# A hybrid decoder layer: where one scan block's outputs stand, and how the last two row tiles are normalised and stored

## The chip, the cores and the metric

The kernel runs on one core of one Trainium2 chip. The core has a matrix engine (TensorE, PE in the profile, with PEld for its weight loads), a vector engine (VectorE, DVE), a scalar engine (ScalarE, ACT), GpSimd (POOL) and SyncE (SP), which issues most transfers. Each engine works through its own instructions in their order; semaphores make one wait for another. The metric is the device time of one execution in microseconds, the median of several runs.

## The reference

One layer over 1024 positions of width 1024, then a final norm, all in float32:

```python
xn = rmsnorm(h, norm_gain)
proj = xn @ w_in                              # 1024 x 3072
u_ssm, z_ssm, h_conv, b_conv, c_conv, z_conv = columns of proj, 512 each
y_ssm = s5_mixer(u_ssm, ...) * silu(z_ssm)    # 32 groups x 64 complex states, scan over positions,
                                              # Re(C s) + D u, gelu, then y * sigmoid(y @ w_glu + b_glu)
y_conv = b_conv * causal_conv3(c_conv * h_conv) * silu(z_conv)
h = h + concat(y_ssm, y_conv) @ w_out
return rmsnorm(h, final_norm_gain)            # h * rsqrt(mean(h*h) + eps) * gain, row by row
```

## The kernel before

Products run as three matmul passes over a high and a low part of each operand (`h`, `x`, `l` in `project`). The first stage loads and normalises x and projects the scan's input. Its order is a table written by hand (`START`) and isn't touched.

The second stage has 16 convolution units and four scan blocks of 8 groups. Its order is the table `ORDER` (L36). A number n is a unit: `conv_hc` or `conv_bz` of channel block n // 4 and half n % 2; units 4 and 5 are `conv_hc` of block 1, unit 6 is `conv_bz`. Of scan block b, `p` prepares coefficients on DVE (`ssm_prep`), `m` and `q` build matrices (`ssm_inject`, `ssm_lags`, tiles `ps_w` and `ps_k`), `i` scans (`ssm_in`, tile `ps_s`; run at high priority, so its work moves ahead in every engine's row), and `o` makes the outputs (`ssm_out`). `ssm_out` has, for each of two halves of the groups, 8 small products into a PSUM tile `ps_y` (L593, L594), then GELU steps on ACT and DVE (L598 to L602), and at its end a store to a scratch tensor in DRAM (L603). A scheduler gives each engine its row of instructions from this order, with the dependencies; the PE row follows it closely, and work of DVE and ACT is interleaved. `ps_w`, `ps_k`, `ps_s` and `ps_y` share the four banks of the PSUM pool `psm` in turn; the results of `project` have four banks of their own (`pmm`). Blocks with an even number keep their scratch (`u2`, `xa`, `xb`, `w1`) in parts of `ysb`, the odd ones in a pool, so block 2 reuses block 0's.

The third stage gates the scan's outputs (`glu`, `gate_z`) and prepares parts of `w_out`. The last stage multiplies by `w_out` with a seven-product scheme over pairs of row tiles (128 rows each) and halves of the columns: T1 to T4 and S1 to S4 are its sums and differences. It loops over four pairs j. A pair's two tiles are `xa` and `xb`, loaded with x as the residual; each product lands in PSUM, `add` (L823, DVE) adds it to a half of a tile (`lo_` and `hi_`, 512 columns), and `final_square` (L826, ACT) sums the squares of a finished half. `rsqrt_steps` (L92 to L98) makes the row factor r from these sums in nine small DVE steps, and `finish` (L842, L843) multiplies a tile by r and the gain `g2b` in one DVE instruction and stores it from SP. The second tile of the last pair goes another way: its final product is computed in two quarters of 256 columns, POOL multiplies each piece by the gain as it comes (`xg`, L879 and L886), and r is applied in halves, one on ACT (L890) and one on DVE (L891), each with a store of its own, from SP (L892) and from ACT's queue (L893).

Of the kernel before, what the change touches and what calls it, by code (L numbers as in the profile page):

```python
# [13 lines left out]
AF = mybir.ActivationFunctionType  # L14
ALU = mybir.AluOpType
MUL, ADD, SUB = ALU.mult, ALU.add, ALU.subtract
# [16 lines left out]
START = ("s0 w0 n0 c s1 W0 n1 W1 w1 t0 L0 g0 L1 U010hl x0 u010x. W2 s2 s3 W3 L2 n23 u20hx u30hx t1 L3 g1 u230l. s4 x1 s5 n45 "  # L33
         "U01231h u01lx. k00 p0 u11lx. k10 t2 u21lx. k20 u31lx. k30 d12 g2 s6 x2 s7 C n67 d12 U01232h u01232l t3 g3 d8 x3 u01232x. "
         "U01233h u03l p1 p2 u03x. k01 u13lx. k11 d u23lx. k21 u33lx. k31")
ORDER = "p0 0 1 2 m0 q0 i0 3 p1 4 o0 5 6 m1 q1 i1 7 p2 8 o1 9 m2 q2 i2 10 p3 11 o2 m3 q3 i3 12 13 o3 14 15"  # L36
MAGIC = 12582912.0
LOG2E = 1.4426950408889634

# [18 lines left out]
def hybrid_kernel(ctx: ExitStack, tc, x, norm_gain, w_in, a_re, a_im, log_dt, b_re, b_im,  # L58
                  c_re, c_im, d_skip, w_glu, b_glu, conv_w, w_out, final_gain, out):
    nc = tc.nc  # L60
    V, A, Q, PE = nc.vector, nc.scalar, nc.gpsimd, nc.tensor
# [10 lines left out]
    out_ci = out[0].rearrange("(c i) d -> c i d", i=T)  # L72
# [11 lines left out]
    ysb = big.tile([P, NB, L], F32, tag="ys", name="ysb")  # L84
# [3 lines left out]
    def rsqrt_steps(parts):  # L88

        vh, y, t = (const.tile([P, 1], F32, tag=f"rs_{q}", name=f"{q}_{rsqrt_steps.n}", bufs=4) for q in ("vh", "y", "t"))  # L90
        rsqrt_steps.n += 1
        ops = [lambda: V.tensor_scalar(vh, parts[0], 0.5 / D, 0.5 * EPS, MUL, ADD)]  # L92
        for part in parts[1:]:
            ops.append(lambda part=part: V.scalar_tensor_tensor(vh, part, 0.5 / D, vh, MUL, ADD))
        ops.append(lambda: V.tensor_scalar(y.bitcast(I32), vh.bitcast(I32), -0.5, 1593268703.0, MUL, ADD))
        for _ in range(3):
            ops.append(lambda: V.scalar_tensor_tensor(t, y, vh, y, MUL, MUL))
            ops.append(lambda: V.scalar_tensor_tensor(y, t, 1.5, y, SUB, MUL, reverse0=True))  # L98
        return ops, y
# [544 lines left out]
    prep, inj, lags, st = {}, {}, {}, {}  # L644
    for what in ORDER.split():
        n = int(what.lstrip("pmiqoz"))
# [42 lines left out]
    g2b = ph3.tile([P, D], F32, name="g2b", bufs=1)  # L689
# [34 lines left out]
    def rows(op, j, home):  # L724

        a, b = (slice(j * 256 + m * P, j * 256 + m * P + P) for m in range(2))
        view = {"A11": cy[:, :, a], "A21": cy[:, :, b], "A12": ysb[:, :, a], "A22": ysb[:, :, b]}
        home = home.rearrange("p m (k c) -> p m k c", k=NB)
        aq[op, j] = home
        if op[0] == "A":  # L730
            t = view[op]
        else:
            t = temp(f"{op}{j}").rearrange("p (k c) -> p k c", k=NB)
            one, two = {"S1": ("A21", "A22"), "S2": ("S1", "A11"), "S3": ("A11", "A21"), "S4": ("A12", "S2")}[op]
            one, two = (view[m] if m in view else aq["raw", m, j] for m in (one, two))
            V.tensor_tensor(t, one, two, ADD if op == "S1" else SUB)
            aq["raw", op, j] = t
        split(home[:, 0], home[:, 1], t)
# [69 lines left out]
    def load_res(j):  # L808
        for m in range(2):
            xr[j, m] = (ph3, wst)[m].tile([P, D], F32, tag="wr", name=f"xr{j}{m}", bufs=2)  # L810
            nc.sync.dma_start(xr[j, m], x_ci[:, 2 * j + m, :])

    lo_, hi_ = slice(0, 512), slice(512, D)

    def mult(ps, op_a, op_b, j, first, cols=slice(0, 512)):
        out_ = ps[:, 0:cols.stop - cols.start]
        for m, (p, q) in enumerate(((0, 0), (0, 1), (1, 0))):
            for k in range(NB):
                PE.matmul(out_, aq[op_a, j][:, p, k], bq[op_b, k][:, q, cols], start=first and m + k == 0,  # L819
                          stop=m == 2 and k == NB - 1, skip_group_check=True)  # L820

    def add(x, ps):
        V.tensor_tensor(x, x, ps, ADD)  # L823

    def final_square(x, acc):
        A.activation(temp(f"sq{final_square.n}")[:, 0:x.shape[-1]], x, AF.Square, accum_out=acc)  # L826
        final_square.n += 1
# [4 lines left out]
    def first_product(j):  # L832
        pw[j] = pmm.tile([P, 512], F32, tag="mm", name=f"ow{j}")
        mult(pw[j], "A11", "B11", j, True)
        add(xr[j, 0][:, lo_], pw[j])

    def finish(j, m, parts):
        x = xr[j, m]
        ops, r = rsqrt_steps(parts)
        for op in ops:  # L840
            op()
        V.scalar_tensor_tensor(x, x, r, g2b, MUL, MUL)  # L842
        nc.sync.dma_start(out_ci[:, 2 * j + m, :], x)  # L843
# [3 lines left out]
    for j in pairs:  # L847
        last = j == pairs[-1]
        xa, xb = xr[j, 0], xr[j, 1]
        part = ph3.tile([P, 5], F32, tag="ss2", name=f"ssp{j}")  # L850
        pz, px = (psm.tile([P, 512], F32, tag="sm", name=f"o{m}{j}") for m in "zx")
        if not last:
            load_res(j + 1)
        mult(pz, "S1", "T1", j, True)
        add(xb[:, hi_], pz)
        mult(pw[j], "S2", "T2", j, False)
        add(xa[:, hi_], pw[j])
        if not last:
            for op in ("A11", "S1", "S2", "S4", "S3", "A12", "A22"):
                rows(op, j + 1, next(homes_a))  # L860
        mult(pz, "S4", "B22", j, False)
        add(xa[:, hi_], pz)
        final_square(xa[:, hi_], part[:, 0:1])
        mult(pw[j], "S3", "T3", j, False)
        add(xb[:, hi_], pw[j])
        final_square(xb[:, hi_], part[:, 2:3])
        mult(px, "A12", "B21", j, True)
        add(xa[:, lo_], px)
        final_square(xa[:, lo_], part[:, 1:2])
        finish(j, 0, [part[:, 0:1], part[:, 1:2]])  # L870
        if not last:
            first_product(j + 1)
            mult(pw[j], "A22", "T4", j, False)
            add(xb[:, lo_], pw[j])
            final_square(xb[:, lo_], part[:, 3:4])
            finish(j, 1, [part[:, 2:3], part[:, 3:4]])
            continue
        xg = ysb[:, 0]
        Q.tensor_tensor(xg[:, hi_], xb[:, hi_], g2b[:, hi_], MUL)  # L879
        steps, r = rsqrt_steps([part[:, 2:3], part[:, 3:4], part[:, 4:5]])  # L880
        for q in range(2):
            c = slice(q * 256, q * 256 + 256)
            mult(pw[j][:, c], "A22", "T4", j, False, c)
            add(xb[:, c], pw[j][:, c])
            final_square(xb[:, c], part[:, 3 + q:4 + q])
            Q.tensor_tensor(xg[:, c], xb[:, c], g2b[:, c], MUL)  # L886
            steps.pop(0)()
        for step_ in steps:
            step_()
        A.activation(xb[:, hi_], xg[:, hi_], AF.Copy, scale=r)  # L890
        V.tensor_scalar_mul(xb[:, lo_], xg[:, lo_], r)  # L891
        nc.sync.dma_start(out_ci[:, 2 * j + 1, lo_], xb[:, lo_])  # L892
        nc.scalar.dma_start(out_ci[:, 2 * j + 1, hi_], xb[:, hi_])  # L893
    ph3.release()
    ph2.release()

# [28 lines left out]
```

## Time and profile before

| what | value |
|---|---|
| median of three runs (lowest, highest) | 437.37 us (437.13, 706.63) |
| the profiled execution | 435.54 us |
| its span, first to last instruction | 433.7 us |
| granted TensorE clock in it | 0.993 |
| PE, DVE, ACT, POOL busy | 96%, 76%, 42%, 7% |
| DMA, mean over the span | 113 GB/s |

The span is what the trace covers; the rest of an execution's time lies around it. Times in the rows count from the span's start. A row of the timeline has start, duration, engine, line, operation, output <- inputs, shape and count, and in brackets how long the engine had been idle before it and who ended that. "SPq" and "ACTq" are the parts of SP and ACT that issue transfers and wait on semaphores. The highest of the three runs stands far above the other two and plays no part in the median.

### The profile page before, as it was taken

What the parts mean: (1) busy time and instruction counts of PE and PEld (TensorE: products, weight loads), DVE (VectorE), ACT (ScalarE), POOL (GpSimd) and SP (SyncE); (2) the same over time, 40 slices, a digit from 0 to 9 for tenths busy, and PEclk for the clock granted to TensorE, in tenths of its full rate; (3) what the DMA queues carried; (4) which work ended last, traced back from release to release, by engine and by line L of the source; (5) the groups of instructions that cost most, each with busy time, mean ns of one, the idle gap of its engine ahead of it and who ended that gap; (6) DMA issues with size and microseconds to landing.
All of it is one profiled execution on the core that took longest, in us unless ns stands there. A gap on an engine that the chain in (4) does not pass through costs nothing. (4 is left out here: it accounts for less than half of the span.)

```text
span 433.7 us, 6302 instructions
## 1 busy us (share of the span) xinstructions
PE 418.2 (96%) x2226; PEld 358.1 (83%) x2226; DVE 331.2 (76%) x821; ACT 181.6 (42%) x322; POOL 32.0 (7%) x39
## 2 busy tenths in 40 slices
PE   8998999999997999999999999999999999999991
PEld 8898999888887888888888888888888888888881
DVE  4973888969989979986996928746456799977734
ACT  4754933074213245135324414647434654333121
POOL 0000003001020020100021000211202100000011
PEclk9999999999999999999999999999999999999997
DMA  7983005433260641254025422577534540333212
GB/s 240 251 256 80 19 2 158 134 91 105 54 166 3 175 116 47 77 147 146 6 47 147 117 81 75 180 200 237 122 109 74 143 123 2 117 125 103 92 48 99
DMA packets 49472, 48.97 MB, mean 113 GB/s; under 512 B 6696, under 2 KB 39488, under 8 KB 49440
## 3 DMA queue, kind: packets, MB, share of 16 engines
q1 hardware_dynamic: 47568, 45.16, 35.5%
q0 software_dynamic: 1728, 3.15, 4.2%
q8 instruction: 17, 0.28, 0.3%
q10 hardware_dynamic: 144, 0.26, 0.2%
q14 instruction: 15, 0.12, 0.1%
HBM read 31.65 MB, written 8.39 MB: 92 GB/s over the span
## 5 line engine op out<-in xcount | busy, mean ns | idle before, releaser
L826 ACT ACTIVATE sq<-xr 128x512 f32<-128x512 f32 (+1 forms) x17 | 10.3, 606 | 41.8 <-DVE xr L823 30.1
L641 POOL TENSOR_TENSOR cy<-cy,sg 128x512 f32<-128x512 f32 x8 | 13.8, 1725 | 187.8 <-DVE sg L640 154.9
L747 PE MATMUL glu<-shl,wg 128*128 128x512 f32 x96 | 21.9, 389 | 0.0
L747 PEld LDWEIGHTS glu<-shl,wg 128*128 128x128 f32 x96 | 18.0, 188 | 3.7
L224 DVE SCALAR_TENSOR_TENSOR xl<-ps_x,g,xh 128x256 fp32r<-128x256 f32 x32 | 12.9, 474 | 8.6 <-ACT xh L218 8.6
L230 PE MATMUL mm_u<-xh,whu 128*128 128x256 f32 x128 | 17.5, 288 | 1.7 <-ACT xh L218 1.7
L230 PEld LDWEIGHTS mm_u<-xh,whu 128*128 128x128 f32 x128 | 16.2, 191 | 2.4 <-ACT xh L218 2.1
L230 PE MATMUL mm_u<-xh,wlu 128*128 128x256 f32 x128 | 17.9, 285 | 0.0
L230 PE MATMUL mm_u<-xl,whu 128*128 128x256 f32 x128 | 17.5, 284 | 0.0
L819 PE MATMUL ow<-bs,ax 128*128 128x512 f32 (+1 forms) x54 | 16.9, 367 | 0.5 <-DVE xr L823 0.5
L230 PE MATMUL mm_h<-xh,wlh 128*128 128x512 f32 x64 | 16.5, 394 | 0.0
L230 PE MATMUL mm_b<-xh,whb 128*128 128x512 f32 x64 | 16.5, 397 | 0.0
L230 PEld LDWEIGHTS mm_u<-xh,wlu 128*128 128x128 f32 x128 | 16.3, 191 | 0.1
L230 PEld LDWEIGHTS mm_u<-xl,whu 128*128 128x128 f32 x128 | 16.2, 192 | 0.1
L230 PE MATMUL mm_h<-xh,whh 128*128 128x512 f32 x64 | 16.1, 391 | 0.0
L230 PE MATMUL mm_b<-xl,whb 128*128 128x512 f32 x64 | 15.9, 390 | 0.0
L230 PE MATMUL mm_h<-xl,whh 128*128 128x512 f32 x64 | 15.8, 389 | 0.0
L230 PE MATMUL mm_c<-xh,whc 128*128 128x512 f32 x64 | 15.8, 389 | 0.0
L230 PE MATMUL mm_z<-xh,wlz 128*128 128x512 f32 x64 | 15.8, 389 | 0.0
L230 PE MATMUL mm_c<-xl,whc 128*128 128x512 f32 x64 | 15.8, 389 | 0.0
L230 PE MATMUL mm_z<-xl,whz 128*128 128x512 f32 x64 | 15.8, 389 | 0.0
L230 PE MATMUL mm_zs<-xh,wlzs 128*128 128x512 f32 x64 | 15.8, 389 | 0.0
(351 smaller groups left out, 1108.3 us busy)
## 6 DMA issues: line engine op xcount, KB each, us to landing
ee<-ec SPq DMA_DIRECT2D x16, 256.0 KB
wro<-in_w_out_dram SPq DMA_DIRECT2D x8, 512.0 KB
xr<-in_x_dram SPq DMA_DIRECT2D x8, 512.0 KB
out_dram<-xr SPq DMA_DIRECT2D x7, 512.0 KB
x<-in_x_dram SPq DMA_DIRECT2D x6, 512.0 KB
wrh<-in_w_in_dram SPq DMA_DIRECT2D x4, 512.0 KB
wrc<-in_w_in_dram SPq DMA_DIRECT2D x4, 512.0 KB
uscr<-us SPq DMA_DIRECT2D x32, 64.0 KB
```

Of the source, the lines that this page charges most:

```text
L224: V.scalar_tensor_tensor(xl[pair // 2][:, kt, n], ps, g1[:, kt:kt + 1], hs.bitcast(F32), MUL, SUB)
L230: PE.matmul(ps[:, n], a[:, kt], b[half][:, kt, n], start=what == "h" and kt == 0, stop=last and kt == KT - 1)
L641: Q.tensor_tensor(yb[:, n], yb[:, n], sg, MUL)
L747: PE.matmul(ps, wg[:, a, k, es], shl[half][:, y, k], start=m + k == 0, stop=m == 2 and k == NB - 1)
L819: PE.matmul(out_, aq[op_a, j][:, p, k], bq[op_b, k][:, q, cols], start=first and m + k == 0, stop=m == 2 and k == NB - 1, skip_group_check ...
L826: A.activation(temp(f"sq{final_square.n}")[:, 0:x.shape[-1]], x, AF.Square, accum_out=acc)
```

## The change

Two things change. In `ORDER`, the outputs of scan block 0 (`o0`) stand behind unit 5 instead of behind unit 4. And in the last pair, `finish` is no longer called for the first tile. POOL multiplies that tile by the gain too, in halves as they are finished (`ga`), ACT applies r to the whole tile in one instruction (L886 after), and SP stores it. The second tile's POOL products are in `gb`. Both of its last stores are issued by SP, the `lo_` half first, and none by ACT.

```diff
-ORDER = "p0 0 1 2 m0 q0 i0 3 p1 4 o0 5 6 m1 q1 i1 7 p2 8 o1 9 m2 ...
+ORDER = "p0 0 1 2 m0 q0 i0 3 p1 4 5 o0 6 m1 q1 i1 7 p2 8 o1 9 m2 ...
...
         final_square(xa[:, lo_], part[:, 1:2])
-        finish(j, 0, [part[:, 0:1], part[:, 1:2]])
         if not last:
+            finish(j, 0, [part[:, 0:1], part[:, 1:2]])
             first_product(j + 1)
...
-        xg = ysb[:, 0]
-        Q.tensor_tensor(xg[:, hi_], xb[:, hi_], g2b[:, hi_], MUL)
+
+        ga, gb = ysb[:, 0], ysb[:, 1]
+        Q.tensor_tensor(ga[:, hi_], xa[:, hi_], g2b[:, hi_], MUL)
+        Q.tensor_tensor(gb[:, hi_], xb[:, hi_], g2b[:, hi_], MUL)
+        Q.tensor_tensor(ga[:, lo_], xa[:, lo_], g2b[:, lo_], MUL)
+        ops, r = rsqrt_steps([part[:, 0:1], part[:, 1:2]])
+        for op in ops:
+            op()
+        A.activation(xa, ga, AF.Copy, scale=r)
+        nc.sync.dma_start(out_ci[:, 2 * j, :], xa)
         steps, r = rsqrt_steps([part[:, 2:3], part[:, 3:4], part[:, 4:5]])
         for q in range(2):
...
-            Q.tensor_tensor(xg[:, c], xb[:, c], g2b[:, c], MUL)
+            Q.tensor_tensor(gb[:, c], xb[:, c], g2b[:, c], MUL)
             steps.pop(0)()
         for step_ in steps:
             step_()
-        A.activation(xb[:, hi_], xg[:, hi_], AF.Copy, scale=r)
-        V.tensor_scalar_mul(xb[:, lo_], xg[:, lo_], r)
-        nc.sync.dma_start(out_ci[:, 2 * j + 1, lo_], xb[:, lo_])
-        nc.scalar.dma_start(out_ci[:, 2 * j + 1, hi_], xb[:, hi_])
+        V.tensor_scalar_mul(xb[:, lo_], gb[:, lo_], r)
+        A.activation(xb[:, hi_], gb[:, hi_], AF.Copy, scale=r)
+        for c in (lo_, hi_):
+            nc.sync.dma_start(out_ci[:, 2 * j + 1, c], xb[:, c])
```

How this moves instructions is seen at three places. First PE, around the outputs of block 0. `mm_h_1711` and `mm_c_1738` are the two products of unit 5, `ps_y_1682` is the first half of the outputs. Before:

```order
L230 MATMUL mm_h_1711<-xh_85,whh_1619 128x512 x8
L230 MATMUL mm_h_1711<-xl_87,whh_1619 128x512 x8
L230 MATMUL mm_h_1711<-xh_85,wlh_1620 128x512 x3
L593 MATMUL ps_y_1682<-ysb,tp_1199 128x128
L594 MATMUL ps_y_1682<-ysb,vv_1203 128x127
```

After, where unit 5's products are `mm_h_1682` and `mm_c_1709`, and the outputs `ps_y_1740`:

```order
L230 MATMUL mm_h_1682<-xh_85,wlh_1620 128x512 x8
L230 MATMUL mm_c_1709<-xh_85,whc_1625 128x512 x8
L230 MATMUL mm_c_1709<-xl_87,whc_1625 128x512 x8
L230 MATMUL mm_c_1709<-xh_85,wlc_1626 128x512 x8
L593 MATMUL ps_y_1740<-ysb,tp_1199 128x128
L594 MATMUL ps_y_1740<-ysb,vv_1203 128x127
```

The outputs stood inside the last pass of unit 5's first product; they now stand behind the whole of unit 5, 29 matmuls later.

Second, DVE in the same stretch. L599, L600 and L602 are the GELU steps of the two halves of block 0's outputs, L106 the low parts of later weights, L500 and L503 coefficients of block 2, L618 to L626 the convolution of unit 5, L636 the first step of unit 6. Before:

```order
L602 TENSOR_TENSOR ysb<-ysb,ps_y_1682 128x512
L517 TENSOR_TENSOR ec_1579<-ec_1579,te_1580 128x8x64
L600 TENSOR_TENSOR ysb<-ysb,ps_y_1696 128x512
L500 TENSOR_TENSOR tv_1971<-bs,apr 128x8x128
L106 TENSOR_TENSOR wlc_2026<-wrc_2023,whc_2025 128x1024
L602 TENSOR_TENSOR ysb<-ysb,ps_y_1696 128x512
L618 TENSOR_TENSOR vp_1616<-hs_1736,mm_c_1738 128x512
L503 TENSOR_TENSOR vv_1970<-c_156,ap 128x1152
L623 COPY vp_1616<-vp_1616 128x2x127
L626 SCALAR_TENSOR_TENSOR cy<-vp_1616,cw,cy 128x1024 x2
L636 TENSOR_TENSOR cy<-cy,mm_b_1781 128x512
```

After:

```order
L623 COPY vp_1616<-vp_1616 128x2x127
L599 TENSOR_SCALAR ysb<-ysb 128x512
L503 TENSOR_TENSOR vv_1970<-c_156,ap 128x1152
L600 TENSOR_TENSOR ysb<-ysb,ps_y_1740 128x512
L626 SCALAR_TENSOR_TENSOR cy<-vp_1616,cw,cy 128x1024
L602 TENSOR_TENSOR ysb<-ysb,ps_y_1740 128x512
L626 SCALAR_TENSOR_TENSOR cy<-vp_1616,cw,cy 128x1024
L599 TENSOR_SCALAR ysb<-ysb 128x512
L636 TENSOR_TENSOR cy<-cy,mm_b_1781 128x512
L600 TENSOR_TENSOR ysb<-ysb,ps_y_1754 128x512
L622 MEMSET vp_2016 128x2
L602 TENSOR_TENSOR ysb<-ysb,ps_y_1754 128x512
```

The GELU steps stood ahead of unit 5's convolution and now stand between its steps and behind unit 6's first. The second L602 is the instruction that gives the second `ps_y` bank free.

Third, ACT at the end. `xr_3746` is the last pair's first tile, `xr_3748` its second, `y_` their row factors. Before:

```order
L826 ACTIVATE sq_3972,ssp_3900<-xr_3746 128x512
L826 ACTIVATE sq_4005,ssp_3900<-xr_3748 128x256
L826 ACTIVATE sq_4022,ssp_3900<-xr_3748 128x256
L890 ACTIVATE xr_3748<-ysb,y_3990 128x512
L893 DMA out_dram<-xr_3748 128x512
```

After:

```order
L826 ACTIVATE sq_3972,ssp_3900<-xr_3746 128x512
L826 ACTIVATE sq_4007,ssp_3900<-xr_3748 128x256
L886 ACTIVATE xr_3746<-ysb,y_3978 128x1024
L826 ACTIVATE sq_4024,ssp_3900<-xr_3748 128x256
L899 ACTIVATE xr_3748<-ysb,y_3992 128x512
```

The first tile's scaling stands on ACT in front of the second tile's last square, and ACT issues no transfer any more. On DVE the only row that goes at this place is L842 on the first tile, ahead of the last L823; POOL has two products of 128x512 more (L880 and L882), and SP has two stores of 128x512 (L901) where it had one.

More of the change, by code (lines that the diff above doesn't have):

```diff
@@ L35 @@
          "U01233h u03l p1 p2 u03x. k01 u13lx. k11 d u23lx. k21 u33lx. k31")
-ORDER = "p0 0 1 2 m0 q0 i0 3 p1 4 o0 5 6 m1 q1 i1 7 p2 8 o1 9 m2 q2 i2 10 p3 11 o2 m3 q3 i3 12 13 o3 14 15"
+ORDER = "p0 0 1 2 m0 q0 i0 3 p1 4 5 o0 6 m1 q1 i1 7 p2 8 o1 9 m2 q2 i2 10 p3 11 o2 m3 q3 i3 12 13 o3 14 15"
 MAGIC = 12582912.0
```

## The prediction

> **What bounds the kernel now.** I read the summary of the page first, then the waits of TensorE (PE), then the rows in order of time at the two places that the change touches: the outputs of the first scan block (128 to 160 us) and the last 14 us.
>
> ```profile
> span 433.7 us, 6302 instructions
> PE 418.2 (96%) x2226; PEld 358.1 (83%) x2226; DVE 331.2 (76%) x821; ACT 181.6 (42%) x322; POOL 32.0 (7%) x39
> ```
>
> PE is busy for 418.2 of 433.7 us, so nearly every microsecond outside the last stage is PE's, and a change there is worth only what it takes from PE's idle time. The view of PE's waits says how much that is:
>
> ```profile
> PE ps_y L594 <- DVE ysb L583: 2.2, 1, 2.2
> ...
> PE ow L819 <- DVE xr L823: 0.5, 1, 0.5
> ```
>
> (Columns: total, times, longest.) The largest single wait is 2.2 us, in `ps_y`, the outputs of a scan block. The other idle time is the stage behind PE's last product, where PE has nothing left:
>
> ```profile
> 423.95 0.28 PE L819 MATMUL ow<-b32wh,ax 128*128 128x256 f32 x1
> ```
>
> (Columns: start, duration.) PE ends at 424.23, and the span at 433.7: 9.5 us of vector work, stores and closing. The execution as a whole took 435.54 us, 1.8 us more than its span; the median of the runs shown is 437.37, again 1.8 above. I work out a difference and subtract it from both.
>
> **Part 1: outputs of scan block 0 after unit 5.** Rows of PE, then the row of VectorE (DVE) that it waited for:
>
> ```profile
> 133.28 0.84 PE L230 MATMUL mm_h<-xh,wlh 128*128 128x512 f32 x3
> ...
> 135.74 0.39 PE L593 MATMUL ps_y<-ysb,tp 128*128 128x128 f32 x2
> 138.33 0.49 PE L594 MATMUL ps_y<-ysb,vv 128*128 128x127 f32 x2 [2.20 <-DVE ysb L583]
> ...
> 139.91 1.41 PE L230 MATMUL mm_h<-xh,wlh 128*128 128x512 f32 x5
> 141.16 1.98 PE L230 MATMUL mm_c<-xh,whc 128*128 128x512 f32 x8
> ```
> ```profile
> 137.58 0.69 DVE L583 TENSOR_TENSOR ysb<-ysb 128x512 f32<-128x512 f32 x1
> ```
>
> PE stands still from 136.13 to 138.33, until the scanned states of the second half are written (137.58 + 0.69 = 138.27). Unit 5's remaining work (5 matmuls of `mm_h`, 24 of `mm_c`, spaced by 1.81/8 = 0.23 us as the starts 139.91 and 141.16 bear out) is 29 x 0.227 = 6.6 us that needs none of this. With it in front, the outputs begin at 133.96 + 6.6 = 140.5, 2.3 us after their input is there. The wait goes: **-2.2 us on PE** if nothing takes its place. No instruction is added or removed here.
>
> What is late next? The GELU steps behind the outputs (L599, L600, L602, twice each on DVE, L598 and L601 on ACT) come later in DVE's row, between the convolution steps of units 5 and 6.
>
> ```profile
> 149.15 0.68 DVE L602 TENSOR_TENSOR ysb<-ysb,ps_y 128x512 f32<-128x512 f32 x1
> ...
> 153.12 2.61 DVE L626 SCALAR_TENSOR_TENSOR cy<-vp,cw,cy 128x1024 f32<-128x1024 f32 x2 [1.22 <-ACT cy L624]
> ...
> 156.47 0.06 DVE L509 MEMSET ec<- 128x4 f32 x1
> ...
> 158.37 0.69 DVE L640 TENSOR_TENSOR sg<-sg,mm_z 128x512 f32<-128x512 f32 x1 [1.61 <-ACT sg L639]
> ```
> ```profile
> 147.00 0.63 ACT L601 ACTIVATE ysb<-ysb 128x512 f32<-128x512 f32 x1 [0.95 <-DVE ysb L600]
> ```
> ```profile
> 158.45 1.26 PE L544 MATMUL ps_k<-vv,bb 128*16 128x128 f32 x10
> 159.65 2.05 PE L569 MATMUL ps_s<-u,w 128*128 128x128 f32 x16
> ```
>
> DVE's same instructions up to L509 lose the 1.22 us wait for ACT's L624, because L599 to L602 now stand between L623 and L626. They gain one: the second L602 follows its L600 with only a memset between, so it waits for ACT's L601, some 0.6 us. L509 thus comes at 156.47 - 1.22 + 0.6 = 155.9, and the second L602 just before it, about 155.9, where it ended at 149.83. This is what hangs on the move: the four PSUM banks of `psm` go round, and the bank of the second `ps_y` tile is that of the second `ps_k` tile of block 1. Its first matmul is in the row at 158.45, some 1 us in, and 2.2 earlier now: 157.2. The margin falls from 9.6 us (159.4 - 149.83) to 1.3 us, but stays a margin. L640 waited for a sigmoid behind PE's `mm_z`, which also comes 2.2 earlier (156.2), and DVE is free by then. Queued behind SP's moved issues (load of block 2's inputs, store of block 0's) nothing is needed before block 2. I take **-2.15**, between 0 (the wait reappears later) and -2.2.
>
> **Part 2: the last pair.** Before, on DVE and ACT:
>
> ```profile
> 420.63 0.69 DVE L823 TENSOR_TENSOR xr<-xr,ox 128x512 f32<-128x512 f32 x1 [1.04 <-PE ox L819]
> 422.06 0.42 DVE L823 TENSOR_TENSOR xr<-xr,ow 128x256 f32<-128x256 f32 x1 [0.74 <-PE ow L819]
> ...
> 422.77 0.54 DVE L97 SCALAR_TENSOR_TENSOR t<-y,vh 128x1 f32<-128x1 f32 x1
> ...
> 423.54 0.22 DVE L97 SCALAR_TENSOR_TENSOR t<-y,vh 128x1 f32<-128x1 f32 x1
> ...
> 424.25 0.16 DVE L98 SCALAR_TENSOR_TENSOR y<-t,y 128x1 f32<-128x1 f32 x1
> 424.44 1.28 DVE L842 SCALAR_TENSOR_TENSOR xr<-xr,y,g2b 128x1024 f32<-128x1024 f32 x1
> 425.64 0.41 DVE L823 TENSOR_TENSOR xr<-xr,ow 128x256 f32<-128x256 f32 x1
> 426.69 0.19 DVE L94 SCALAR_TENSOR_TENSOR vh<-ssp,vh 128x1 f32<-128x1 f32 x1 [0.63 <-ACT sq L826]
> ...
> 428.25 0.16 DVE L98 SCALAR_TENSOR_TENSOR y<-t,y 128x1 f32<-128x1 f32 x1
> 428.51 0.49 DVE L891 TENSOR_SCALAR xr<-ysb,y 128x512 f32<-128x512 f32 x1
> ```
> ```profile
> 426.15 0.42 ACT L826 ACTIVATE sq<-xr 128x256 f32<-128x256 f32 x1 [3.07 <-DVE xr L823]
> ...
> 428.85 0.72 ACT L890 ACTIVATE xr<-ysb,y 128x512 f32<-128x512 f32 x1 [2.19 <-issue]
> 429.60 1.44 ACTq L893 DMA_DIRECT2D out_dram<-xr  x1
> ```
> ```profile
> L624 ACT ACTIVATE cy<-vp,cw x4: 1149/1153/1154, 95.2 to 257.6; 128x1024 f32<-128x1024 f32 x4
> ```
> ```profile
> 418.74 1.29 POOL L879 TENSOR_TENSOR ysb<-xr,g2b 128x512 f32<-128x512 f32 x1 [68.47 <-DVE xr L823]
> 422.56 0.74 POOL L886 TENSOR_TENSOR ysb<-xr,g2b 128x256 f32<-128x256 f32 x1 [2.53 <-DVE vh L94]
> ```
>
> *DVE.* L842 goes from in front of the last addition, which moves from 425.64 to about 424.5. That looks like 1.1 us, but ACT now has the first tile's scaling (128x1024) ahead of the last square, and the square is what the chain needs.
>
> *Pool.* Of its two new products beside DVE's work, the one at 416.0 is alone. The low half follows the addition of 420.63 + 0.69: 421.4 to 422.7. The addition of 422.06, which lets PE's last product go on, then lies inside it. Does Pool hold it up? The nearest rows are an addition with one operand in PSUM inside a Pool product:
>
> ```profile
> 123.34 2.35 POOL L641 TENSOR_TENSOR cy<-cy,sg 128x512 f32<-128x512 f32 x1 [15.49 <-DVE sg L640]
> ```
> ```profile
> 124.44 0.69 DVE L572 TENSOR_TENSOR ysb<-ps_s,ee 128x512 f32<-128x512 f32 x1
> ```
>
> L572 takes its usual 0.69 there, so no; bounds 0 to 0.6 (422.70 against 422.06), and I take 0. The small step L97, however, took 0.54 instead of 0.22 and ended (423.31) with Pool's product (422.56 + 0.74). That product starts 0.15 later now, behind the new one, so r of the first tile comes at 424.41 + 0.15 = 424.56 (bounds 0 and +0.4).
>
> *ACT.* It starts 0.09 to 0.44 after its last input (rows 425.64 to 426.15, 428.25 to 428.85) and takes 1.15 (L624), at most twice 0.72. In the middle: 424.56 + 0.27 + 1.2 = 426.03. The square follows at 426.0 instead of 426.15: **-0.15**, between -0.45 and +0.5. L94 no longer meets Pool (0.19 to 0.15), so r of the second tile, the last L98 and L891 come 0.2 earlier. The first tile's store starts at 426.05 instead of 425.75; its transfer is over before the next begins.
>
> *The last stores.*
>
> ```profile
> 429.03 0.33 SPq L892 DMA_DIRECT2D out_dram<-xr  x1
> ```
> ```profile
> DMA  0000020089999710100000999896000000000000
> ```
> ```profile
> SPq L920 <- DMA out_dram<-xr: 3.0, 2, 2.5
> ```
>
> The second fence is the DMA share between 428.9 and 433.7, 0.12 us to a digit. The half that SP issues at 429.03 moves from 429.86 to 430.6, beginning 0.83 after its issue. The half that ACT issues at 429.60, in 1.44 instead of 0.33 us, begins at 431.54 (1.94 after) and ends at 432.4; the rest is receipt and closing. From SP, with everything 0.2 earlier: ready at 429.4, packets from 430.25, but behind the other half until 430.4, and 0.86 long: 430.4 to 431.3 instead of 432.4. With the 0.2 in it, this is **-1.1** for the whole tail (the bounds of the square give -1.4 to -0.4; a late receipt gives 0, below).
>
> [...]
>
> **Sum:** -2.15 - 1.1 = -3.25 us, 0.7%: 435.54 would become 432.3, and the median 437.37 **434.1**.
>
> **Rivals.**
> *The end gives nothing.* The slow start belongs to the last transfer, not to ACT's queue: then the second SP store also begins 1.94 after issue. Or its receipt is late: SP's longest wait in the last fence, 2.5 us, was for the first half, long after that half's packets were through. Either way -0.2 remains of the tail: -2.35, **435.0**. For it: one sample of each queue. Against: the SP rows are all 0.33.
> *DVE takes the place.* In the 17 us behind the outputs DVE has little idle time (1.22 and 1.61), and L602, L640 or L106 run late; half of part 1 or all of it is lost: -1.1 to -2.2, about **435.8**. Against: DVE still finds two waits there that are PE's or ACT's.
> *Slower.* The bank of the second `ps_y` tile: if DVE's second L602 slips past 157.2, PE stands at `ps_k`, and with it L569 and all of block 1's scan behind it, microsecond for microsecond. The kernel is slower than before only from a slip of 1.3 + 3.25 = 4.55 us on; at 5.5 it is **438.3**. DVE would need four more waits like that of 1.22.
>
> **How the numbers follow.** Both gains about whole (433.6 to 434.9): 0.58. The end gives nothing: 0.2. DVE takes the place: 0.14. Slower: 0.05. Something beyond 433.6: 0.03. The first three reach to 436.3, and the profiled execution lay 1.8 below the median, so the runs themselves spread by that: 432.6 to 436.8. Two per cent (8.7 us), about what a measurement of this kernel can tell from no change, lie outside every case: faster 0.02, within 0.96, slower 0.02.
>
> **What would show it.** Right: no wait of PE at `ps_y`, none at `ps_k` of block 1; `mm_b` of unit 6 at about 144.4 (146.6 before); the last add near 424.5, the last square near 426.0; two issues of 0.33 on SP and the closing some 1 us closer to PE's end. Wrong: a new PE wait in 155 to 190 us on DVE; a second store with a long issue or a gap in front; ACT's scaling past 426.4.

## The result, and the profile after

The changed kernel took 432.88 us (median of four runs, 431.56 to 433.97) beside 437.25 for the kernel before in the same rounds: a ratio of 0.9917, 95% interval 0.9893 to 0.9942. In a second set of rounds it was 433.72 beside 437.03, 0.9919 (0.9891 to 0.9947). The forecast was 434.1, a ratio of 0.9925. The profiled execution took 432.44 us against 435.54. The page of the changed kernel:

```profile
span 430.7 us, 6302 instructions
PE 418.2 (97%) x2226; PEld 358.0 (83%) x2226; DVE 330.1 (77%) x820; ACT 182.5 (42%) x323; POOL 34.6 (8%) x41
```

In sum PE is busy as long as before, and the 3.0 us that went are idle time; but the sum hides two changes of the busy time that cancel, and both show below. Cut at three instructions, the two traces compare like this (the last column is behind PE's last product):

| us | start to unit 5 | unit 5 to `mm_b` of unit 6 | `mm_b` to PE's last product | last product to the end |
|---|---|---|---|---|
| before | 129.66 | 16.95 | 277.62 | 9.51 |
| after | 130.48 | 14.37 | 277.78 | 8.05 |
| difference | +0.82 | **-2.58** | +0.16 | **-1.46** |

The sum is -3.06, the difference of the spans. The two stretches that the change touches make -4.04 of it. The +0.82 at the start comes from the clock that TensorE was granted: between 60 and 70 us its mean was 1.00 before and 0.83 after, and PE got through 75 matmuls there instead of 87. At 61 us the changed kernel's PE was 0.25 us ahead of before's, at 67 us 1.04 behind. (A row has start and end, length, then the busy time of PE with its instructions, of weight loads, DVE, ACT and POOL, and last the granted clock, the DMA share and GB/s; before, then after.)

```profile
60.00:70.00 10.00, 10.00 (x87) 9.93 (x86) 9.18 (x42) 6.07 (x12) 1.42 (x5) 1.00 0.19 51
```
```profile
60.00:70.00 10.00, 10.00 (x75) 9.88 (x75) 8.41 (x39) 6.06 (x12) 0.94 (x3) 0.83 0.15 38
```

In these traces the instructions ahead of unit 5 stand on PE in the same order; what else is known of this drop stands further down. The view of PE's waits after, all its rows:

```profile
PE mm_u L230 <- ACT xh L218: 1.7, 2, 1.1
PE ps_warm L182 <- POOL ident masks.py:199: 1.4, 1, 1.4
PE ps_x L211 <- DVE x L203: 0.6, 1, 0.6
PE ow L819 <- DVE xr L823: 0.5, 1, 0.5
```

The wait at `ps_y` is gone, and none stands at `ps_k`. The second column, seen in the busy time of the stretch, before and then after:

```profile
129.66:146.60 16.94, 14.74 (x81) 12.66 (x80) 16.49 (x50) 5.62 (x9) 0.00 (x0) 1.00 0.18 55
```
```profile
130.48:144.84 14.36, 14.36 (x81) 12.49 (x80) 13.90 (x45) 4.44 (x6) 0.00 (x0) 1.00 0.13 38
```

The same 81 matmuls: before, 2.20 us idle and 14.74 busy; after, never idle and 14.36 busy. The neighbours of the moved outputs in the timeline after:

```profile
155.28 0.63 ACT L601 ACTIVATE ysb<-ysb 128x512 f32<-128x512 f32 x1 [3.89 <-DVE vp L622]
155.94 0.69 DVE L602 TENSOR_TENSOR ysb<-ysb,ps_y 128x512 f32<-128x512 f32 x1 [0.69 <-ACT ysb L601]
...
156.78 0.68 DVE L640 TENSOR_TENSOR sg<-sg,mm_z 128x512 f32<-128x512 f32 x1
```
```profile
156.81 1.26 PE L544 MATMUL ps_k<-vv,bb 128*16 128x128 f32 x10
```

The second L602 does wait for ACT's L601 (0.69 us) and gives its bank free at 156.63; PE needs it some 1 us into the `ps_k` row, about 157.8. And the end, ACT and then SP, after:

```profile
423.05 1.15 ACT L886 ACTIVATE xr<-ysb,y 128x1024 f32<-128x1024 f32 x1 [1.57 <-DVE y L98]
424.11 0.40 ACT L826 ACTIVATE sq<-xr 128x256 f32<-128x256 f32 x1
...
426.36 0.72 ACT L899 ACTIVATE xr<-ysb,y 128x512 f32<-128x512 f32 x1 [1.76 <-DVE y L98]
```
```profile
424.23 0.33 SPq L887 DMA_DIRECT2D out_dram<-xr  x1
426.95 0.81 SPq L901 DMA_DIRECT2D out_dram<-xr  x2
```
```profile
SPq L928 <- DMA out_dram<-xr: 1.5, 2, 0.9
```

PE's last product ends at 422.63, so the last square stands 1.48 behind it (1.92 before) and the issue of the first of the two last stores 4.32 (4.80 before). SP then waits 1.5 us in all for the stores, 3.0 before.

### The profile page after: what moved, and what is told of

Its sections match the earlier page's. It is cut to its first block, busy times and chain, and to the rows that moved or that the text cites. A ratio compares the mean times of both kernels' runs of the same rounds, so it can differ in the third digit from the quotient of the medians.

```text
span 430.7 us, 6302 instructions
## 1 busy us (share of the span) xinstructions
PE 418.2 (97%) x2226; PEld 358.0 (83%) x2226; DVE 330.1 (77%) x820; ACT 182.5 (42%) x323; POOL 34.6 (8%) x41
## 4 chain that ended last, share of the span: by engine, by line
PE 95%; DMA 2%; DVE 1%; ACT 1%; issue 1%; SPq 1%; ACTq 0%
PE mm_u L230 11%; PE mm_b L230 10%; PE mm_h L230 10%; PE mm_z L230 10%; PE mm_c L230 10%; PE mm_zs L230 10%; PE ow L819 10%; PE oz L819 5%; PE glu L747 5%; PE ox L819 3%; PE ps_s L569 2%; PE ps_k L544 2%; PE ps_y L593 2%; DMA wru<-in_w_in_dram 2%; PE ps_y L594 2%; PE ps_x L211 1%
```

## The experiments

Times behind "PE's last product" are from the end of its last matmul to the named point; landings are the trace's records of a store's 16 parts.

**One half of the change at a time.** First the order alone, on the kernel before:

```diff
-ORDER = "p0 0 1 2 m0 q0 i0 3 p1 4 o0 5 6 m1 ...
+ORDER = "p0 0 1 2 m0 q0 i0 3 p1 4 5 o0 6 m1 ...
```

> The order table alone is changed (block 0's outputs behind unit 5); the end is as before. My theory: PE's wait of 2.2 us at ps_y goes and nothing takes its place. From the first unit-5 matmul to the first matmul of unit 6 it took 16.94 us before (129.66 to 146.60) and 14.36 us with the whole change (130.48 to 144.84); I expect 14.4 here, no wait at ps_y or ps_k, and 2.2 to 2.6 us off the time: about 434.8 against 437.25. Rival 'DVE takes the place': a new wait of PE on DVE between 150 and 190 us and less than 1.2 us off. Rival 'the end gives it all': no difference.

Measured: 435.02 us beside 436.29, ratio 0.9969 (0.9952 to 0.9987). Unit 5 to `mm_b` 14.37, no wait at `ps_y` or `ps_k`. The end stayed long, 9.82: ACT's issue took 1.51 us, and 0.2 us more than before went by in the closing, where a last instruction of DVE (DRAIN) came at 9.46 instead of 9.03. Then the ending alone, with `ORDER` as before:

```diff
-        finish(j, 0, [part[:, 0:1], part[:, 1:2]])
         if not last:
+            finish(j, 0, [part[:, 0:1], part[:, 1:2]])
...                                   # and the rest of the ending as in the changed kernel
```

> The end alone is changed (POOL products of the first tile, its scaling on ACT, both last stores from SP); the order table is as before. My theory: PE keeps its 2.2 us wait at ps_y, and from PE's last matmul to the end of the span it takes 8.05 us as with the whole change, 9.5 before: 1.1 to 1.5 us off, about 435.9. [...]

Measured: 435.64, ratio 0.9985 (0.9967 to 1.0003), an interval that takes in no change; the end 8.24, with 0.2 of it from that late instruction of DVE, as in the run before. Each half thus does its work in the trace without the other. In the times the halves come to less (-1.3 and -0.65) than in the traces and than expected. One reason is the wait itself, which isn't the same in every execution of the old order. Here it was

```profile
PE ps_y L594 <- DVE ysb L583: 1.4, 1, 1.4
```

instead of 2.2. Over the six profiled executions with the old order it was 1.4 to 2.2 us, and the stretch from unit 5 to `mm_b` 16.13 to 16.95: always the wait plus 0.37 to 0.40 above 14.37. The move is worth 1.8 to 2.6 us. Another may be the start: the traces of both halves have the drop of the clock, before's has not, and up to unit 5 they took 131.25 and 131.84 us instead of 129.66.

**Which queue issues the last store.** The changed kernel with the last store back on ACT's queue, and the kernel before with it on SP:

```diff
-        for c in (lo_, hi_):
-            nc.sync.dma_start(out_ci[:, 2 * j + 1, c], xb[:, c])
+        nc.sync.dma_start(out_ci[:, 2 * j + 1, lo_], xb[:, lo_])
+        nc.scalar.dma_start(out_ci[:, 2 * j + 1, hi_], xb[:, hi_])
```

> The whole change, but the last half tile is stored from ACT's queue, as before. My theory, that the slow issue belongs to ACT's queue: the issue takes about 1.4 us again, its packets begin 1.9 us after it, and from PE's last matmul to the end of the span it takes 0.7 to 1.0 us more than with the whole change (8.05), so 433.7 against 432.9. [...]

```diff
-        nc.scalar.dma_start(out_ci[:, 2 * j + 1, hi_], xb[:, hi_])
+        nc.sync.dma_start(out_ci[:, 2 * j + 1, hi_], xb[:, hi_])
```

> The kernel before, with one edit: the last half tile is stored from SP. My theory: the second issue on SP takes 0.33 us, its packets follow the first half's, and the end after PE's last matmul shrinks from 9.5 to about 8.5 (1.0 us off, 436.2). Rival 'the slow start belongs to the last transfer': the second SP issue takes 1.4 us too and the end stays within 0.2 of 9.5.

Measured: 433.35 (0.9935, 0.9911 to 0.9959) and 436.11 (0.9998, 0.9982 to 1.0015). ACT's issue in the changed kernel, and SP's second one in the kernel before:

```profile
427.60 0.37 ACTq L901 DMA_DIRECT2D out_dram<-xr  x1
```
```profile
428.42 0.33 SPq L892 DMA_DIRECT2D out_dram<-xr  x1
428.99 0.48 SPq L893 DMA_DIRECT2D out_dram<-xr  x1
```

ACT's queue isn't slow: 0.37 us, and the end is 8.04 as with SP (8.05). With SP in the old ending it stays at 9.44 (9.51). The theory fell in both traces. In the old ending with SP the first half landed at 8.01 and the second at 8.41, late without any long issue. Something else holds the old ending.

**What holds it: transfers named "instruction".** A trace lists a queue of that name (q14) with transfers of 8 KB. Three fall near the end: in before at 4.47, 5.30 and 6.64 behind PE's last product, in the changed kernel at -7.06, 1.79 and 8.68. The queues while the last stores are under way, before (429.0 to 432.7) and after (426.9 to 429.6); a row has packets, MB and the share of the 16 DMA engines' time, and q10 has packets only where ACT issues a store:

```profile
q1 hardware_dynamic: 144, 0.26, 18.9%
q10 hardware_dynamic: 144, 0.26, 18.4%
q14 instruction: 2, 0.02, 1.3%
```
```profile
q1 hardware_dynamic: 288, 0.52, 50.9%
```

The trace has their times, sizes and the queue's name; that they fetch the engines' next instructions, as my expectations have it, was my guess. If so, their place depends on how many instructions an engine has had. So the kernel before got spare instructions near its start, on ACT alone and on DVE alone, with the ending untouched:

```diff
+    spare = const.tile([P, 1], F32, name="spare")
+    for _ in range(8):
+        A.copy(spare, sgn)
```

> The kernel before with eight more instructions on ACT near the program's start (a copy of one column each), so that everything behind stands eight places later in ACT's instruction stream. Theory: the late end of the kernel before comes from instruction fetches, the 8 KB transfers of the queue named instruction, which fall at 4.47, 5.30 and 6.64 us behind the last matmul in before (at -7.06, 1.79 and 8.68 in the changed kernel); the one at 5.30 is ACT's, and ACT's DMA issue (1.44 us, against 0.37 in the changed kernel with the last store on ACT) waits for it. With ACT's stream shifted that fetch falls ahead of 2 us, the issue takes 0.37 to 0.45 and last matmul to the span's end goes from 9.51 to 8.4-8.8. Rival: the issue is long because of what ACT or the queue does there (a first transfer on that queue behind SP's); then it stays at 1.4 to 1.5 and the stretch at 9.4 to 9.8.

```diff
+    spare = const.tile([P, 1], F32, name="spare")
+    for _ in range(16):
+        V.memset(spare, 0.0)
```

> The kernel before with sixteen more instructions on DVE near the program's start (a memset of one column each, while DVE is idle), which shift DVE's instruction stream by sixteen places. Theory of the fetches, with DVE's fetch as one of those at 4.47 and 6.64 us behind the last matmul: it goes to about -1 us or earlier; the last share of the lo_ half's store then lands at 7.0 instead of 8.0, while ACT's issue stays at 1.44 and the end at 9.4 to 9.8, since the hi_ half lands last. If neither fetch moves, DVE has no part in the end. Rival without fetches: nothing moves at all.

ACT's rows with ACT shifted, and with DVE shifted (line numbers are 3 higher than before's):

```profile
429.05 0.72 ACT L893 ACTIVATE xr<-ysb,y 128x512 f32<-128x512 f32 x1 [1.91 <-DVE y L101]
429.80 0.46 ACTq L896 DMA_DIRECT2D out_dram<-xr  x1
```
```profile
428.74 0.72 ACT L893 ACTIVATE xr<-ysb,y 128x512 f32<-128x512 f32 x1 [2.19 <-issue]
429.49 1.42 ACTq L896 DMA_DIRECT2D out_dram<-xr  x1
```

Shifting ACT took away both the idle 0.3 us that the profile calls "issue" ahead of ACT's last scaling and the long DMA issue (1.44 to 0.46); the transfer at 5.30 was gone, and the three now stood at 3.92, 4.21 and 6.65 (not ahead of 2 us, as I had it). Shifting DVE did neither, but the transfer at 6.64 was gone (to -9.47), and the last part of the first store landed at 6.93 instead of 8.00. Yet the end was 9.45 and 9.50: each time the other late thing still held it. As forecast for DVE; for ACT the forecast of 8.4 to 8.8 was wrong. The run with the order alone says the same of DVE without any spare instruction: it has 961 recorded instructions of DVE instead of 962, the transfer stood at 10.12, and the last part of the first store landed at 7.08. Then both shifts together:

> The kernel before with both shifts at once: eight more instructions on ACT and sixteen more on DVE near the start. Each alone removed one of two late things (ACT's issue went from 1.44 to 0.46 us; the last share of the lo_ half landed at 6.93 instead of 8.00 us behind the last matmul) and the end stayed at 9.45 and 9.50, because the other one still held it. Theory of the fetches: together lo_ has landed by 7.0 and hi_ by 7.3-7.6, and last matmul to the span's end goes from 9.51 to 8.3-8.6 us; in the time 0.8 to 1.2 us below before, less what ACT's eight instructions cost at the start. Rival: some third thing holds the end at 9.4 to 9.5 and the two signs were side effects.

Measured: the end 8.52, and 435.53 us beside 437.03, ratio 0.9966 (0.9944 to 0.9988), for 24 more instructions that do nothing for the result. That is 1.5 us less, for 0.8 to 1.2 expected, with an interval of 0.5 to 2.4. The queues in the same stretch (429.6 to 432.4), and SP's wait:

```profile
q1 hardware_dynamic: 144, 0.26, 25.2%
q10 hardware_dynamic: 144, 0.26, 24.4%
```
```profile
SPq L925 <- DMA out_dram<-xr: 2.0, 2, 1.4
```

No such transfer is left there (two stand just ahead of it, at 3.92 and 4.21); the halves have landed at 6.87 and 7.50 (8.00 and 8.48 before). The reverse, four spare instructions on DVE in the changed kernel (the same memset, four times):

> The changed kernel with four more instructions on DVE near the start. In the kernels before with 962 recorded DVE instructions a fetch stood at 6.64 us behind the last matmul, amid the last stores; with 960 or 961 (the changed kernel, and before with the order alone changed) it came behind the end, at 8.6 and 10.1 us. With 964 theory says that it comes back among the stores (between 3.9 and 6.7 us), and that the last share of one of the two halves lands 0.7 to 1.1 us later: the stretch from the last matmul to the span's end goes from 8.05 to 8.5-9.1 us. Rival: what matters is what the changed ending does, not where its fetches fall; then the stretch stays at 8.0 to 8.1.

```profile
427.57 0.16 DVE L101 SCALAR_TENSOR_TENSOR y<-t,y 128x1 f32<-128x1 f32 x1
428.19 0.48 DVE L901 TENSOR_SCALAR xr<-ysb,y 128x512 f32<-128x512 f32 x1 [0.46 <-DVE y L101]
```
```profile
q1 hardware_dynamic: 288, 0.52, 49.8%
q14 instruction: 1, 0.01, 1.3%
```

The transfer comes back among the stores (4.84), and the end goes from 8.05 to 8.46, just short of the range. The way is another one than I wrote: no part lands late by itself, but DVE pauses 0.46 us ahead of its last scaling, as ACT did before, and both stores go out later.

**The order of ACT's two jobs.** In the changed kernel the square whose result the end hangs on waits for the first tile's scaling. Here it goes first:

```diff
-        A.activation(xa, ga, AF.Copy, scale=r)
-        nc.sync.dma_start(out_ci[:, 2 * j, :], xa)
...                                   # the loop with the last two squares; then
+            A.activation(xa, ga, AF.Copy, scale=r_a)
+            nc.sync.dma_start(out_ci[:, 2 * j, :], xa)
```

> The changed kernel with the first tile's scaling on ACT put behind the last square instead of in front of it. Theory: in the changed kernel the last square starts 1.48 us behind the last matmul because ACT is still in the scaling of 1.15 us (from 0.42 to 1.57); its input is there at 0.59, so it now starts at about 0.65, the row factor and the last two scalings come 0.8 us earlier, and last matmul to the span's end goes from 8.05 to 7.2-7.4 us; the first tile's store starts 0.8 us later and is out of the way in time. In the time: 0.6 to 0.9 us below the changed kernel, 431.8-432.6 beside 437.25 for before. Rival: the first tile's 512 KB now lie in front of the last two stores, whose packets then begin later by the 0.2 to 0.9 us that were won, and the stretch stays at 8.0.

Measured: 432.18 beside 436.75, ratio 0.9885 (0.986 to 0.991). Last square at 0.67, end 7.30:

```profile
425.01 0.42 ACT L826 ACTIVATE sq<-xr 128x256 f32<-128x256 f32 x1 [1.82 <-DVE xr L823]
425.34 0.19 ACT L826 ACTIVATION_READ_ACCUMULATOR sq<-xr 128x1 f32 x1
425.43 1.13 ACT L896 ACTIVATE xr<-ysb,y 128x1024 f32<-128x1024 f32 x1
```

But `mm_b` to PE's last product was 278.86 instead of 277.78. It and the changed kernel ran once more, side by side:

> The kernel with the last square ahead of the first tile's scaling once more, beside the changed kernel. Its end was 0.75 us shorter (7.30), but its last matmul came 1.08 us later behind mm_b of unit 6 than in the changed kernel, where PE waits for a sum on DVE that stands behind a late load of w_out. Theory: that lateness is of the one execution and not of the edit (nothing ahead of the last pair is edited), so that stretch is 277.6-277.9 here; the end is 7.3 again, and the time 0.5 to 0.9 us below the changed kernel's. Rival: the edit changes the order earlier too; then 278.8 again and a time equal to the changed kernel's within 0.3 us.

> The changed kernel once more, unaltered, on the same chip and in the same rounds as the two beside it, so that they can be compared with it directly: 0.988 to 0.994 of before. Start of unit 5 to mm_b of unit 6 is 14.37 us as in every run with the new order, and last matmul to the end 8.04-8.06.

Measured: 433.22 (0.9906, 0.9871 to 0.9941) and 433.72; the ends 7.31 and 8.04; unit 5 to `mm_b` 14.37 in both. Both had 278.66 from `mm_b` to PE's last product, the unaltered changed kernel too, so that the microsecond belongs to the execution (neither of my two numbers for it was right). Its place, in the changed kernel's second trace:

```profile
342.41 0.69 DVE L714 TENSOR_TENSOR T<-wro,T 128x512 f32<-128x512 f32 x1 [0.80 <-DMA wro<-in_w_out_dram]
```

A load of `w_out` arrives in time or late, and PE then waits for DVE's first sum. With the outputs placed as in the change, DVE waits for it in four of seven traces (0.3 to 1.0 us), and `mm_b` to PE's last product is longer in these four by 0.4 to 1.1; with the old order that is so in one of six. Whether the earlier PE makes it more frequent can't be told from so few. The version with the square first has an end shorter by 0.73 to 0.75 us in both traces; the times of the common rounds, -0.5 with overlapping intervals, agree but don't prove it.

**One unit later still.** The outputs of block 0 behind unit 6 (`... p1 4 5 6 o0 m1 ...`):

> The changed kernel with the outputs of scan block 0 one unit later still, behind unit 6, just ahead of the building of block 1's matrices. It asks from which point the later place costs. Theory of the prediction: what decides is whether the PSUM banks of these outputs come free before the next products need them; here the next products (ps_k) come right behind, and the free banks go round in another order, so a wait of PE at ps_k or ps_y of 1 to 4 us appears between 150 and 160 us, and mm_b of unit 6 comes at about the same distance behind unit 5 or earlier by the 1.9 us of the outputs. Rival (DVE is far enough ahead): no wait of PE over 0.5 us between 140 and 165 us, and the stretch from the start of unit 5 to the end of the last matmul stays within 0.5 us of the changed kernel's 292.15 us.

Measured in one run: 432.64; start of unit 5 to PE's last product 292.92 against 292.15, and one wait on the way:

```profile
PE ps_k L544 <- ACT w L532: 0.5, 1, 0.5
```

Neither number held. The wait is there, but small, and it isn't the bank of `ps_y`: PE waits for ACT's copy of `ps_w`. One unit later gains nothing more and, in this one execution, costs 0.8 us in the stretch, of which 0.5 is that wait.

## Why the prediction was right, and where it wasn't

*The sum.* The two parts came to -4.04 us in the traces for -3.25 forecast (-2.58 for -2.15, -1.46 for -1.1). That the two profiled executions differ by -3.06, close to the forecast, is chance: the start, longer by 0.82 with the drop of the clock, stood in no term and took that much back.

*The order.* The mechanism is shown: the wait goes, in every trace with the move, and nothing takes its place. The margin at `ps_k` was 1.2 us (156.63 to 157.8) for 1.3 forecast. With the later start (0.82) taken off, `mm_b` of unit 6 came at 144.02 for 144.4 and L640 at 155.96 for 156.2, L602 as described. The size was -2.58 for -2.15: I took the idle time of the waits' view as the whole cost. The busy time of the stretch shows 0.38 more before; the last matmul ahead of a pause isn't overlapped by the next (rows 0.39 long start 0.22 apart), and the first pair behind it is slower (from 138.33 to the next at 138.65 it is 0.32 instead of 0.22). That makes 0.17 and 0.10; the last 0.11 lies in the five `mm_h` behind the outputs, which took 1.25 us, where 5 x 0.227 is 1.14.

*DVE and POOL at the end.* As forecast: the last addition came 0.17 behind PE's last product (0.27 forecast), the addition of 256 columns beside POOL's product kept its 0.42, and L97 was stretched to 0.48. *ACT.* Here the term was mis-sized: the last square came 0.44 earlier, not 0.15, at the edge of its bounds. It is a sum of small things, each on the good side: r of the first tile 0.25 behind PE's last product instead of 0.33, ACT's start 0.17 after it instead of 0.27, 1.15 us of scaling instead of 1.2, and a square that starts at 424.11, 0.09 before the scaling's row ends. The upper end of my 0.09 to 0.44 for the start was before's row at 428.85, whose "issue" idle was since shown to move with ACT's instruction count.

*The last stores.* Here the step failed. "1.44 us from ACT, 0.33 from SP" was read as a property of the queue; it was that of one place in ACT's instruction stream (0.46 with eight copies put in far ahead). The swap itself moves the end by 0.01 and 0.07 us. With spare instructions that shift the instruction transfers out from among the last stores the old ending takes 8.52 instead of 9.51, so of the -1.46 about 1.0 goes with where these transfers fall, and the remaining 0.47 matches the square's 0.44. That the change moved them (from 4.47, 5.30 and 6.64 to -7.06, 1.79 and 8.68) goes with the instructions it adds and removes: DVE has 960 recorded for 962, ACT 453 for 454. The -1.1 was near by luck: one wrong cause stood in for another. The first rival was right that the slow start isn't that of ACT's queue (0.37 from it in the changed kernel), and its late first half was real too (landed at 8.00), but it wasn't there any more in the changed kernel (6.38).

*The other rivals.* DVE doesn't become the bound: its waits of 1.2 and 1.6 us in that stretch turned into one of 0.7. The bank never held PE.

What stays open: which transfer goes with which engine was my inference, since the trace doesn't name the engine. Besides what moved, the counts speak for it: of the 15 transfers of 8 KB after the start of before's span, four stand at ACT's recorded instructions 63, 194, 321 and 449 (127 to 131 apart), the last of them that at 5.30, and eight at DVE's 52, 184, 311, 450, 566, 705, 834 and 959 (116 to 139 apart), the last of them that at 6.64. The one at 4.47 isn't assigned. That a transfer makes an engine pause isn't shown: the runs show that the two move together.

The start up to unit 5 took 129.3 to 131.8 us over the fourteen traces. What parts them is the granted clock: in the eight traces with 130.4 us and more it was 0.5 for 3.41 us, from a point between 62 and 65 us on; the six with 130.2 and less have no such stretch. In the changed kernel's trace the clock is 1.0 for 58.03 us, 0.5 from 62.35 on for 3.41, and 1.0 again for 361.81; in before's it is 1.0 for 419.84 in one piece. In both PE makes 32 products of 64x64 (`ps_cb`, 3.5 us in all) up to about 63 us. What makes the clock fall isn't shown. Nor do the traces part the drop from the edit: the eight are among the nine with the new order or the new ending, and none of the other five has it. The executions speak for a clock that varies without an edit: of 29 of the kernel before in the rounds of the first four experiments, nine with a mean granted clock of 0.992 or more took 434.9 to 436.1 us, and seventeen with 0.990 or less 435.8 to 438.0. Only their mean clock is on record.

## What to carry to other kernels

Price a wait by the time from start to start across the stretch, not by its idle time alone. Where an engine idles with "issue" as the reason, or a DMA issue is several times its usual length (1.44 us here, 0.46 with eight copies put in ahead), look for the instruction transfers in that window and shift the stream by a few harmless instructions before blaming the queue or the operation. Differences of 1 us in a short ending can come from nothing but instruction counts (9.51 to 8.52 here), so an edit there is judged beside a version with its count shifted. And compare the granted clock stretch by stretch before two traces are compared as a whole: here the longer start hid 0.8 us of what the two edited stretches gave.

## What the runs showed of the hardware that I had not expected

ACT lost 0.33 us ahead of its last scaling and about 1 us in its one DMA issue (1.44, and 0.46 with eight copies put in far ahead); DVE lost 0.46 us ahead of its last scaling in the changed kernel with four memsets more. Both hang on the number of instructions ahead: ACT's pause was gone with the eight copies, and DVE's isn't there without the four memsets. In the same stretches the trace has transfers of 8192 bytes, named instruction (at 5.30 in before, at 4.84 with the four memsets, behind PE's last product). What they bring isn't shown. (A second queue of the same name, q8, moves 16384 bytes at a time, 17 times in before's trace, the last at 396.28 us and so not in the ending.)

The granted clock fell to 0.5 for 3.41 us in the middle of a run, though the profile counts PE as busy all the time around it (10.00 of 10.00 us in the second row of 60 to 70 us). It did so in eight of fourteen traces, in the changed kernel's from 62.35 us on, when the last of 3.5 us of small products stood on PE.
